# Eight value projections as four Winograd-style pairs ahead of the mixers, read back from DRAM

## The chip, the cores and the metric

The kernel runs on one core of a Trainium2 chip. The metric is the device time of one execution in microseconds (us), lowest is best. Engines: TensorE (PE) with its weight loads (PEld), VectorE (DVE), ScalarE (ACT), GpSimd (POOL), and SyncE (SP), which issues all of this kernel's DMAs in one queue of its own. Each engine works through its instructions strictly in order.

## The reference

One layer of a hybrid recurrent decoder: 1024 prompt tokens with 16 learned meta tokens ahead of them, and 8 sample sequences of 4 tokens, 1072 token columns in all, model width 1024. `w_in` makes everything that the four branches and the gates need, from the normalised input:

```python
xn = rmsnorm(h, norm_w)
(gq, gk, gv, glr, gg, hq, hf, hi, hg_g, mq, mk, mv, mi, mf, mo, mg,
 ca, cb, cg, mgate) = split_cols(xn @ w_in)
...
oA = chunked gated linear attention (q = gq, k = gk, v = gv, decay from glr)     # GLA, 4 heads, dk 64, dv 128
zA = head_rmsnorm(oA, gla_norm) * silu(gg)
oB = the same recurrence (q = silu(hq), k = 1 - f, v = hi, decay f from hf)      # HGRN2, 4 heads of 128
zB = head_rmsnorm(oB, hg_norm) * silu(hg_g)
zC = mLSTM branch (mq, mk, mv, mi, mf, mo, mg);  zD = convolution branch (ca, cb, cg)
...
mixed = sum over i of sigmoid(mgate_i) * (z_i @ w_branch[i])
h = h + mixed @ w_out;  y = rmsnorm(h, final_norm)
```

The mixers' states after the prompt and after each sample sequence are outputs too. `gv` and `hi`, the values of the first two branches, are 512 wide each: four blocks of 128 channels.

## The kernel before, in words

Data lie channels first: 128 channels by 1072 tokens (`NT`); the 1056 without meta tokens are `NY`, the 16 meta tokens `NM`. A float32 product is three matmuls of rounded parts, xh·wh, xl·wh and xh·wl (lines 185 to 187, and 280 to 282 in the pairs). ACT rounds the weights to `wh` (L138), POOL or DVE makes the rest `wl` (L139).

**Two ways to make a block of 128 output channels.** Direct (`proj`): three groups of 358, 358 and 356 columns (`GA`) or three of 352 (`GY`), each 8 slices of the depth by three products, 72 matmuls into a PSUM tile `acc`, and an eviction for each group. By pairs (`pair`): two neighbouring blocks at once, with seven half-size products in place of eight (Winograd's form of Strassen's scheme); 56 times three matmuls of at most 268 columns, 168 in all. The half sums of x are made once (`combine_x`), those of the weights for each pair (`ta`, `tb`), and DVE adds the partial sums up. `pair_to` applies a function and writes both blocks to a DRAM scratch (`gscr`, `cscr`, `sscr`), in quarters, without the meta columns.

**Stages.** x is normalised and transposed; four gate blocks and the small projections run directly. Then come 19 pairs in the order of the list `todo`, with the four convolution pairs and their 120 taps on DVE (L392) between the first. x is restored from scratch, and the mixers begin: `hg_unit` 0 to 3 (HGRN2, a head each), `gla_unit` 0 and 1 (GLA, two heads each), `ml_unit` 0 to 3. Last are the branch products and `w_out`.

**A mixer unit.** It projects its blocks directly (hf, hq and the value block hi for HGRN2; gk, gq and two value blocks gv for GLA). `vtok` makes the value block: three evictions by ACT into `vf` (one buffer, L589) and a copy of the sample columns `x9`; nine transposes on PE (`tta`, L546, PSUM tiles shared with `acc`, three buffers) and ACT's copies bring it to tokens first (`vt`, four buffers); one transpose `v9p` serves the samples. `linear_unit` then runs the scan in levels (`lv`, L647: PE, then DVE products q and k, L662 and L663), one or two filler gate blocks (`filler`), the state updates (`ds`, L812), the outputs (`op`, L831, L833, L733, L849), and at its end

- the norm: squares on ACT, sums on DVE (L774, L777), the power on POOL (L117), the product with o on DVE (L749, L751);
- `zt` (L755): nine transposes of o on PE, whose result DVE multiplies into the gate (L763, L758), and a write to `zscr`;
- `sds` (L860): the samples' state products, from masked values `vb` (L739), added to the states on DVE (L861), two for an HGRN2 head and four for a GLA unit.

`zt`, `sds`, `op`, `lv`, `ds` and `cps` come from one pool of three PSUM tiles. `ml_cols` (11 transposes `cps`, L981 to L994, each copied out by DVE) stands in the program between the two GLA units.

**What sets the order.** The program is written unit after unit. The framework's scheduler, with a timeline model of its own, puts every engine's instructions in one fixed list, and in it the end of a unit is interleaved with the next unit's projections:

```python
with tile.TileContext(nc, schedule_with_timeline_sim=True) as tc:
```

Of the kernel before, what the change touches and what calls it, by code (L numbers as in the profile page):

```python
# [12 lines left out]
F32 = mybir.dt.float32  # L13
# [3 lines left out]
AF = mybir.ActivationFunctionType  # L17
# [5 lines left out]
NM, NPR, NSEQ, NDEC = 16, 1024, 8, 4  # L23
NP = NM + NPR
NT = NP + NSEQ * NDEC
NY = NT - NM
D = 1024
P = 128
# [14 lines left out]
GA = [(0, 358), (358, 358), (716, 356)]  # L43
GY = [(16, 352), (368, 352), (720, 352)]
HT = NT // 2
# [20 lines left out]
def trunk(ctx, tc, hx, w_in, w_sm, w_br, w_out, pk, wgk2, mlb, fnorm, s_gla, s_hg, s_c, s_n, s_m, s_cv,  # L66
# [3 lines left out]
    V, S, G, T, DMA = nc.vector, nc.scalar, nc.gpsimd, nc.tensor, nc.sync  # L70

    cst = ctx.enter_context(tc.tile_pool(name="cst", bufs=1))
    dr = ctx.enter_context(tc.tile_pool(name="dr", bufs=1, space=DRAM))
# [39 lines left out]
    def mmt(name):  # L113
        return pools["pm"].tile([P, 512], F32, name=name, tag="mm")
# [9 lines left out]
    cscr = dr.tile([4, P, NY], F32, name="cscr", tag="cscr")  # L124
    xscr = dr.tile([2, P, KH, HT], F32, name="xscr", tag="xscr")
    sscr = dr.tile([16, P, NY], F32, name="sscr", tag="sscr")
    yscr = dr.tile([4, P, NY], F32, name="yscr", tag="yscr")

    def load_raw(src, c0, kd=KD):
        raw = pools["wp"].tile([P, KD, P], F32, name="wraw", tag="wraw")  # L130
        src = src if c0 is None else src[:, c0:c0 + P].rearrange("(k p) m -> p k m", p=P)
        DMA.dma_start(raw[:, :kd], src)
        return raw

    def split_w(raw, kd=KD, E=None, pool="wp"):
        hi = pools[pool].tile([P, KD, P], F32R, name="wh", tag="wh", bufs=2)
        lo = pools[pool].tile([P, KD, P], F32R, name="wl", tag="wl", bufs=2)
        S.activation(hi[:, :kd], raw[:, :kd], AF.Copy)  # L138
        (E or G).tensor_tensor(lo[:, :kd], raw[:, :kd], hi[:, :kd], ALU.subtract)  # L139
        return hi, lo  # L140

    def load_w(src, c0, kd=KD):
        return split_w(load_raw(src, c0, kd), kd)
# [5 lines left out]
    with tc.tile_pool(name="x0", bufs=9, side="right", reuse_waits="tile") as x0:  # L149
# [8 lines left out]
        for i0 in (0, 3, 6):  # L158
# [11 lines left out]
            for k in range(KD):  # L170
                ps = mmt("xt")
                t = 0
# [4 lines left out]
                hi = xh[:, k, i0 * P:i0 * P + t]  # L177
# [11 lines left out]
    def proj_w(hi, lo, groups, evac):  # L189
        for t0, n in groups:  # L190
            ps = acc_tile()
            mm3(ps[:, :n], lambda k: hi[:, k, :], lambda k: lo[:, k, :],
                lambda k: xh[:, k, t0:t0 + n], lambda k: xl[:, k, t0:t0 + n], KD)
            evac(ps[:, :n], t0, n)

    def proj(sec, i, groups, evac):
        hi, lo = load_w(w_in, OFF[sec] + i * P)
        proj_w(hi, lo, groups, evac)
# [9 lines left out]
    def stt(tag, name=None):  # L208
        return gtl(tag, [P, HT], STB[tag], name)
# [42 lines left out]
    def pair(c0, c1, c11, c12, c22, c21, m=0):  # L252

        wp = pools["gph"]
        r0, r1 = load_raw(w_in, c0), load_raw(w_in, c1)
        b11, b21, b12, b22 = r0[:, :KH], r0[:, KH:], r1[:, :KH], r1[:, KH:]
        w1 = split_w(r0)
        ta = wp.tile([P, KD, P], F32, name="ta", tag="tt", bufs=2)  # L260
        t1, t2 = ta[:, :KH], ta[:, KH:]
        V.tensor_tensor(t1, b12, b11, ALU.subtract)
        V.tensor_tensor(t2, b22, t1, ALU.subtract)
        w2 = split_w(ta, E=V, pool="gph")
        tb = wp.tile([P, KD, P], F32, name="tb", tag="tt", bufs=2)
        t3, t4 = tb[:, :KH], tb[:, KH:]
        V.tensor_tensor(t3, b22, b12, ALU.subtract)
        V.tensor_tensor(t4, b21, t2, ALU.subtract)
        w3 = split_w(tb, E=V, pool="gph")
        w4 = split_w(r1[:, KH:], KH)  # L270
        ps = lambda tag: [pools["ps"].tile([P, 512], F32, name="s" + tag, tag="a" if tag == "a" else "r",
                                           bufs=2 if tag == "a" else 5)[:, :HS] for _ in range(2)]

        def prod(w, o, x, s, out, start, stop, m=0):
            m = m if s == 0 else 0
            out = out[:, m:]
            xa, xb = (t[:, :, s * HS + m:(s + 1) * HS] for t in xs[x])
            for k in range(KH):
                wh, wl = w[0][:, o + k], w[1][:, o + k]
                T.matmul(out, wh, xa[:, k], start=start and k == 0, stop=False, skip_group_check=True)  # L280
                T.matmul(out, wh, xb[:, k], start=False, stop=False, skip_group_check=True)  # L281
                T.matmul(out, wl, xa[:, k], start=False, stop=stop and k == KH - 1, skip_group_check=True)  # L282

        h = lambda t, s: t[:, s * HS:(s + 1) * HS]
        a, b, c = ps("a"), ps("b"), ps("c")
        p1, u2 = stt("p1"), stt("u2")
        for s in range(2):
            prod(w1, 0, "a11", s, a[s], True, True)
            S.activation(h(p1, s), a[s], AF.Copy)
        for s in range(2):  # L290
            prod(w2, KH, "s2", s, b[s], True, True)
            V.tensor_tensor(h(u2, s), h(p1, s), b[s], ALU.add)
        p5, u3 = stt("p5"), stt("u3")
        for s in range(2):
            prod(w2, 0, "s1", s, c[s], True, True)
            S.activation(h(p5, s), c[s], AF.Copy)
        for s in range(2):
            prod(w1, KH, "a12", s, a[s], False, True, m)
            c11(s, a[s])
        d = ps("d")  # L300
        for s in range(2):
            prod(w3, 0, "s3", s, d[s], True, True)
            S.activation(h(u3, s), d[s], AF.Copy)
        V.tensor_tensor(u3, u3, p5, ALU.add)
        V.tensor_tensor(u3, u3, u2, ALU.add)
        c22(u3)
        for s in range(2):
            prod(w4, 0, "s4", s, c[s], False, True, m)
            V.tensor_tensor(h(p1, s), h(u2, s), c[s], ALU.add)
        c12(p1)  # L310
        for s in range(2):
            prod(w3, KH, "a22", s, d[s], False, True)
            V.tensor_tensor(h(u2, s), h(u2, s), d[s], ALU.add)
        c21(u2)

    def pair_to(sec, i, dst, func, times=False, base=0):

        g11 = stt("g11")
        o = OFF[sec] + i * P
        i += base  # L320

        def c11(s, ps):
            g = g11[:, s * HS:(s + 1) * HS]
            S.activation(g, ps, func)
            if times:
                V.tensor_tensor(g, ps, g, ALU.mult)  # L326
            if s == 1:
                DMA.dma_start(dst[i, :, 0:HT - NM], g11[:, NM:])

        def rest(j, second):  # L330
            def ev(t):
                if times:
                    sg = stt("sg")
                    S.activation(sg, t, func)
                    V.tensor_tensor(t, t, sg, ALU.mult)
                elif func != AF.Copy:
                    S.activation(t, t, func)
                if second:
                    DMA.dma_start(dst[j, :, HT - NM:], t)
                else:  # L340
                    DMA.dma_start(dst[j, :, 0:HT - NM], t[:, NM:])
            return ev

        pair(o, o + P, c11, rest(i + 1, False), rest(i + 1, True), rest(i, True), NM)

    def conv_pair(i):
        u = gtl("u", [P, UW + NSEQ * 34])
# [100 lines left out]
    for j in range(2, NDIR):  # L448
# [8 lines left out]
    todo = [("gate", i, gscr, AF.Sigmoid) for i in range(NDIR, 32 - NFILL, 2) if i not in LATE]  # L457
    todo += [("cg", i, cscr, AF.Copy) for i in (0, 2)]
    todo += [(sec, i, sscr, AF.Sigmoid, sec != "mo", 4 * n) for n, sec in ((3, "mo"), (0, "gg"), (1, "hg"), (2, "mg"))
             for i in (0, 2)]  # L460
    for i in range(4):
        cu = conv_pair(i)
        pair_to(*todo.pop(0))
        conv_taps(i, *cu)
        pair_to(*todo.pop(0))
        conv_states(i, *cu)
        pair_to(*todo.pop(0))
# [44 lines left out]
    for i in range(2):  # L512
        t = mx.tile([P, 8, P], F32, name=f"att{i}", tag=f"att{i}")
        G.memset(t, 0.0)
        attb.append(t)
        t = mx.tile([TAIL, TAIL], F32, name=f"att8{i}", tag=f"att8{i}")
# [6 lines left out]
    for i in range(2):  # L523
        t = mx.tile([TAIL, P], F32, name=f"attp{i}", tag=f"attp{i}")
# [58 lines left out]
    def vtok(sec, i, ones_col=False):  # L583
        vf = tl("vf", [P, 9 * P], 1)
        G.memset(vf[:, NT:NT + 16], 0.0)
        x9 = tl("x9", [P, 3, NT - NP], 1)

        def ev(ps, t0, n):
            S.activation(vf[:, t0:t0 + n], ps, AF.Copy)  # L589
            if t0 + n == NT:  # L590
                S.activation(x9, ps[:, NP - t0:].unsqueeze(1).broadcast_to([P, 3, NT - NP]), AF.Copy)

        proj(sec, i, GA, ev)
        vt = tl("vt", [P, 9, 129], 4)
        (to_tok_v(vf, vt) if ones_col else to_tok(vf, vt, True))
        v9 = split3(x9, 1, "v9", 4, mmt("v9p"))
        if ones_col:
            G.memset(vt[:, :, 128:129], 1.0)
        return vt, v9
# [669 lines left out]
    for i in range(9):  # L1269
# [24 lines left out]
        dst = yp[t0:t0 + P, :] if i < 8 else ys  # L1294
# [83 lines left out]
```

## Time and profile before

| what | value |
|---|---|
| median of 3 runs | 1569.58 us (1568.48 to 1570.25) |
| the profiled execution's own time | 1570.24 us |
| its span | 1568.5 us |
| mean granted clock of PE | 0.994 |
| instructions | 30293, of them 12471 matmuls |
| DMA | 176.43 MB, mean 112 GB/s |

The span runs from the first to the last instruction of the profiled execution, and the own time is what the device took for it; 1.7 us lie around the span. The page gives each engine's busy time as a share of the span, then the span in 40 slices of 39.2 us with a digit for the busy share, then the chain of work that ended last, and the groups of instructions by line. In rows such as `acc<-xh,wh` the written tile stands left of the arrow and the read ones right. Line numbers are those of the kernel before.

### The profile page before, as it was taken

What the parts mean: (1) busy time and instruction counts of PE and PEld (TensorE: products, weight loads), DVE (VectorE), ACT (ScalarE), POOL (GpSimd) and SP (SyncE); (2) the same over time, 40 slices, a digit from 0 to 9 for tenths busy, and PEclk for the clock granted to TensorE, in tenths of its full rate; (3) what the DMA queues carried; (4) which work ended last, traced back from release to release, by engine and by line L of the source; (5) the groups of instructions that cost most, each with busy time, mean ns of one, the idle gap of its engine ahead of it and who ended that gap; (6) DMA issues with size and microseconds to landing.
All of it is one profiled execution on the core that took longest, in us unless ns stands there. A gap on an engine that the chain in (4) does not pass through costs nothing. (4 is left out here: it accounts for less than half of the span.)

```text
span 1568.5 us, 30293 instructions
## 1 busy us (share of the span) xinstructions
PE 1530.4 (98%) x12471; PEld 1469.8 (94%) x12471; DVE 1039.6 (66%) x1825; ACT 558.8 (36%) x1131; POOL 465.5 (30%) x400
## 2 busy tenths in 40 slices
PE   6999999999999999999999999999999999999998
PEld 5999999999999999999998898999999999999886
DVE  6949989999998547445553666576675556744523
ACT  6543343332333334323522523423333255422311
POOL 2222222232213232223232222223323223877200
PEclk9999999999999999999999999999999999999999
DMA  5432333332337213231323133154333377676221
GB/s 175 136 99 76 97 110 103 96 110 71 95 106 230 56 44 111 57 104 52 109 69 101 37 92 91 58 151 127 110 96 93 105 251 212 189 240 192 95 106 49
DMA packets 195823, 176.43 MB, mean 112 GB/s; under 512 B 14508, under 2 KB 170048, under 8 KB 195684
## 3 DMA queue, kind: packets, MB, share of 16 engines
q1 hardware_dynamic: 195684, 174.49, 36.7%
q8 instruction: 98, 1.61, 0.4%
q14 instruction: 41, 0.34, 0.1%
HBM read 122.45 MB, written 52.00 MB: 111 GB/s over the span
## 5 line engine op out<-in xcount | busy, mean ns | idle before, releaser
L139 POOL TENSOR_TENSOR wl<-wraw,wh 128x512 fp32r<-128x512 f32 (+1 forms) x123 | 279.7, 2276 | 627.2 <-ACT wh L138 600.1
L185 PE MATMUL acc<-xh,wh 128*128 128x352 f32 (+2 forms) x1320 | 437.9, 332 | 2.2 <-ACT xh L178 2.2
L186 PE MATMUL acc<-xl,wh 128*128 128x352 f32 (+2 forms) x1320 | 436.0, 330 | 0.0
L187 PE MATMUL acc<-xh,wl 128*128 128x352 f32 (+2 forms) x1320 | 434.4, 329 | 0.0
L185 PEld LDWEIGHTS acc<-xh,wh 128*128 128x128 f32 x1320 | 250.6, 190 | 6.6 <-ACT xh L178 3.0
L186 PEld LDWEIGHTS acc<-xl,wh 128*128 128x128 f32 x1320 | 250.7, 190 | 1.9
L187 PEld LDWEIGHTS acc<-xh,wl 128*128 128x128 f32 x1320 | 250.2, 190 | 2.1 <-issue 0.7
L392 DVE SCALAR_TENSOR_TENSOR y<-u,pkt,y 128x1024 f32<-128x1024 f32 x120 | 192.7, 1606 | 0.6
L138 ACT ACTIVATE wh<-wraw 128x512 fp32r<-128x512 f32 (+1 forms) x125 | 110.4, 883 | 211.1 <-PE acc L186 116.5
L185 PE MATMUL acc<-zh,wh 128*128 128x352 f32 x384 | 124.6, 324 | 0.3 <-DVE gt L1209 0.3
L186 PE MATMUL acc<-zl,wh 128*128 128x352 f32 x384 | 124.4, 324 | 0.0
L187 PE MATMUL acc<-zh,wl 128*128 128x352 f32 x384 | 124.3, 324 | 0.0
L280 PE MATMUL sa<-xh,wh 128*128 128x268 f32 (+1 forms) x304 | 87.4, 287 | 1.7 <-DVE g L326 1.0
L281 PE MATMUL sa<-xl,wh 128*128 128x268 f32 (+1 forms) x304 | 86.6, 285 | 0.0
L282 PE MATMUL sa<-xh,wl 128*128 128x268 f32 (+1 forms) x304 | 86.6, 285 | 0.0
L1210 POOL TENSOR_TENSOR mix<-mix,gt 128x352 f32<-128x352 f32 x72 | 72.1, 1016 | 28.9 <-DVE gt L1209 25.7
L662 DVE TENSOR_TENSOR q<-q,tot 128x256 f32<-128x256 f32 (+3 forms) x96 | 45.8, 478 | 51.8 <-PE lv L647 51.1
L185 PEld LDWEIGHTS acc<-zh,wh 128*128 128x128 f32 x384 | 72.2, 188 | 1.1 <-issue 0.5
L187 PEld LDWEIGHTS acc<-zh,wl 128*128 128x128 f32 x384 | 72.3, 188 | 0.0
L186 PEld LDWEIGHTS acc<-zl,wh 128*128 128x128 f32 x384 | 72.2, 188 | 0.0
L1209 DVE TENSOR_TENSOR gt<-acc,gt 128x352 f32<-128x352 f32 x72 | 36.1, 517 | 38.6 <-PE acc L187 36.7
L280 PEld LDWEIGHTS sa<-xh,wh 128*128 128x128 f32 x304 | 57.3, 188 | 2.3 <-DVE g L326 1.4
(397 smaller groups left out, 3320.9 us busy)
## 6 DMA issues: line engine op xcount, KB each, us to landing
wraw<-w_in SPq DMA_DIRECT2D x92, 512.0 KB, 4.1
gt<-gscr SPq DMA_DIRECT2D x30, 528.0 KB, 4.9
gscr<-gd SPq DMA_DIRECT2D x60, 176.0 KB, 1.8
zr<-zscr SPq DMA_DIRECT2D x16, 528.0 KB, 4.3
wraw<-w_br SPq DMA_DIRECT2D x32, 256.0 KB, 2.9
gt<-sscr SPq DMA_DIRECT2D x12, 528.0 KB, 5.3
zscr<-gt SPq DMA_DIRECT2D x12, 528.0 KB
sscr<-u SPq DMA_DIRECT2D x16, 268.0 KB, 2.1
```

The costliest lines, as they stand in the source:

```text
L138: S.activation(hi[:, :kd], raw[:, :kd], AF.Copy)
L139: (E or G).tensor_tensor(lo[:, :kd], raw[:, :kd], hi[:, :kd], ALU.subtract)
L185: T.matmul(ps, wh(k), ah(k), start=(i == 0), stop=False)
L186: T.matmul(ps, wh(k), al(k), start=False, stop=False)
L187: T.matmul(ps, wl(k), ah(k), start=False, stop=(i == kd - 1))
L280: T.matmul(out, wh, xa[:, k], start=start and k == 0, stop=False, skip_group_check=True)
L281: T.matmul(out, wh, xb[:, k], start=False, stop=False, skip_group_check=True)
L282: T.matmul(out, wl, xa[:, k], start=False, stop=stop and k == KH - 1, skip_group_check=True)
L392: V.scalar_tensor_tensor(ymain, u[:, NM + j:NM + j + NPR], w(j), ymain, ALU.mult, ALU.add)
L662: V.tensor_tensor(qx[:, :, 1], qx[:, :, 1], pv[r, :, 0:1].broadcast_to([rw, nb, h]), ALU.mult)
L1209: V.tensor_tensor(gt[:, t0:t0 + n], ps[:, :n], gt[:, t0:t0 + n], ALU.mult)
L1210: G.tensor_tensor(mixed[j][:, t0:t0 + n], mixed[j][:, t0:t0 + n], gt[:, t0:t0 + n], ALU.add)
```

## The change

The eight value blocks of the HGRN2 and GLA units (`hi` and `gv`) are made in four more pairs, the last four of `todo`, with all 1072 columns (`m` = 0), and written to a new scratch `vscr`. `vtok` loads `vf` from there with one DMA of 128 x 1072 on SP's queue, and makes `x9` from `vf`; the direct projection stays for the mLSTM values alone. The number of weight blocks that are loaded, rounded and split stays the same. On PE 576 direct matmuls go and 672 of a pair's width come; ACT loses 24 evictions `vf<-acc`.

```diff
+    vscr = dr.tile([8, P, NT], F32, name="vscr", tag="vscr")
...
-    def pair_to(sec, i, dst, func, times=False, base=0):
+    def pair_to(sec, i, dst, func, times=False, base=0, m=NM):
...
-                DMA.dma_start(dst[i, :, 0:HT - NM], g11[:, NM:])
+                DMA.dma_start(dst[i, :, 0:HT - m], g11[:, m:])
...
-                    DMA.dma_start(dst[j, :, HT - NM:], t)
+                    DMA.dma_start(dst[j, :, HT - m:], t)
                 else:
-                    DMA.dma_start(dst[j, :, 0:HT - NM], t[:, NM:])
+                    DMA.dma_start(dst[j, :, 0:HT - m], t[:, m:])
...
-        pair(o, o + P, c11, rest(i + 1, False), rest(i + 1, True), rest(i, True), NM)
+        pair(o, o + P, c11, rest(i + 1, False), rest(i + 1, True), rest(i, True), m)
...
+    VB = {"hi": 0, "gv": 4}
+    todo += [(sec, i, vscr, AF.Copy, False, VB[sec], 0) for sec in VB for i in (0, 2)]
...
-        proj(sec, i, GA, ev)
+        if sec in VB:
+            DMA.dma_start(vf[:, :NT], vscr[VB[sec] + i])
+            S.activation(x9, vf[:, NP:NT].unsqueeze(1).broadcast_to([P, 3, NT - NP]), AF.Copy)
+        else:
+            proj(sec, i, GA, ev)
```

The rows of the order below carry the changed kernel's own line numbers, which are up to 7 higher (`zt` L762 for L755, `tta` L549 for L546, `lv` L654 for L647, the products L186 to L188 for L185 to L187), and numbers behind the names that count tiles; behind a row stands what it waits for.

**The end of an HGRN2 unit, on PE.** The first unit's last output matmul is followed, before, by 63 matmuls of projections, the next unit's value block among them; then its `zt`:

```order
L187 MATMUL acc_6700<-xh_96,wl_6643 128x352
L185 MATMUL acc_6700<-xh_96,wh_6642 128x352
L186 MATMUL acc_6700<-xl_97,wh_6642 128x352
L755 MATMUL zt_6470<-ident_70,o_6420 128x128 [waits DVE_49,PE_49]
L755 MATMUL zt_6470<-ident_70,o_6420 128x128 x3
```

In the changed kernel 40 matmuls of projections and eight transposes of the next unit's loaded value block stand there:

```order
L187 MATMUL acc_7526<-xl_98,wh_7468 128x352
L188 MATMUL acc_7526<-xh_97,wl_7469 128x352
L549 MATMUL tta_7561<-ident_70,vf_7555 128x128 [waits DMAHW6_49,DVE_49]
L549 MATMUL tta_7561<-ident_70,vf_7555 128x128 x3
L549 MATMUL tta_7567<-ident_70,vf_7555 128x128 [waits DVE_49]
L549 MATMUL tta_7567<-ident_70,vf_7555 128x128 x3
L762 MATMUL zt_7296<-ident_70,o_7246 128x128 [waits DVE_49,Activation_49]
L762 MATMUL zt_7296<-ident_70,o_7246 128x128 x3
```

Behind the second and the third unit's outputs it was 51 and 61 matmuls, and is 30 and 42 with eight transposes.

**The two value blocks of the first GLA unit, on PE.** Before, the transposes of the first block (`vf_9334`) are followed by the 72 matmuls of the second block, of which the first few are shown, and only then by its transposes:

```order
L546 MATMUL tta_9435<-ident_70,vf_9334 48x128 [waits Activation_49]
L565 MATMUL v9p_9438<-ident_70,x9_9336 96x128 [waits PE_49]
L185 MATMUL acc_9452<-xh_96,wh_9448 128x358 [waits Activation_49]
L186 MATMUL acc_9452<-xl_97,wh_9448 128x358
L187 MATMUL acc_9452<-xh_96,wl_9449 128x358 [waits Pool_49]
```

Now the load of the second block (`vf_9937`, into the one buffer that `vf_9911` held) has the rest of the level and the fourth HGRN2 unit's `zt` ahead of its transposes:

```order
L549 MATMUL tta_9929<-ident_70,vf_9911 48x128 [waits Activation_49]
L654 MATMUL lv_10017<-q_9722,k_9733 32x32 [waits DVE_49]
L654 MATMUL lv_10017<-q_9722,k_9733 32x32 x9
L762 MATMUL zt_9689<-ident_70,o_9639 128x128 [waits DVE_49]
L762 MATMUL zt_9689<-ident_70,o_9639 128x128 x3
L762 MATMUL zt_9695<-ident_70,o_9639 128x128 [waits DVE_49]
L762 MATMUL zt_9695<-ident_70,o_9639 128x128 x3
L762 MATMUL zt_9701<-ident_70,o_9639 128x128 [waits DVE_49]
L549 MATMUL tta_9943<-ident_70,vf_9937 128x128 [waits DMAHW0_49]
```

In the second GLA unit the second load stands likewise, with 31 `lv`, two `ds` and seven `op` of the first unit in between, and the first unit's other 35 outputs behind it.

**The end of the first GLA unit, on PE.** Before, its state products and the `cps` transposes are spread over the next unit's two value blocks; each `sds` has projection matmuls ahead of it and behind it:

```order
L186 MATMUL acc_10578<-xl_97,wh_10522 128x356
L187 MATMUL acc_10578<-xh_96,wl_10523 128x356
L185 MATMUL acc_10578<-xh_96,wh_10522 128x356
L860 MATMUL sds_10174<-vb_10175,k9_10000 128x512 [waits DVE_49,PE_49]
L981 MATMUL cps_10180<-ident_70,ct_6506 128x96 [waits PE_49]
```

Now they follow each other:

```order
L867 MATMUL sds_10570<-vb_10571,k9_10411 128x512 [waits DVE_49]
L867 MATMUL sds_10575<-vb_10576,k9_10411 128x512 [waits DVE_49]
L867 MATMUL sds_10580<-vb_10581,k9_10411 128x512 [waits DVE_49,PE_49]
L867 MATMUL sds_10585<-vb_10586,k9_10411 128x512 [waits DVE_49,PE_49]
L988 MATMUL cps_10591<-ident_70,ct_7332 128x96 [waits PE_49]
L988 MATMUL cps_10594<-ident_70,ct_7332 128x96 [waits DVE_49]
L988 MATMUL cps_10597<-ident_70,ct_7332 128x96 [waits DVE_49]
```

## The prediction

> **What bounds the kernel now.** The page comes first: busy shares, the slices of the span, the chain that ended last.
>
> ```profile
> span 1568.5 us, 30293 instructions
> PE 1530.4 (98%) x12471; PEld 1469.8 (94%) x12471; DVE 1039.6 (66%) x1825; ACT 558.8 (36%) x1131; POOL 465.5 (30%) x400
> PE   6999999999999999999999999999999999999998
> DVE  6949989999998547445553666576675556744523
> PE 23%; DVE 1%; DMA 1%; issue 0%; ACT 0%; DVEq 0%; POOLq 0%; SPq 0%; POOL 0%; ACTq 0%
> ```
>
> TensorE (PE) is busy in 98% of the span, in every slice but the ends, and the part of the chain that the profile follows is PE's. So two sums count: how many matmul columns go away, and how long PE stands still in its fixed order at the places from which they are taken. DVE is full in the first 12 slices (pairs and convolution) and half idle in the mixers. Then come PE's timeline for the price of a pair and of a direct block, and the timelines of PE, DVE and POOL where a unit ends, for what the removed blocks covered. Rows give start, duration, line, operation, and in brackets the idle time before with its releaser.
>
> **The change part by part.** *Pairs against direct blocks.*
>
> ```profile
> 473.73 0.39 PE L280 MATMUL sa<-xh,wh 128*128 128x268 f32 x1 [0.50 <-DVE g L326]
> 494.44 0.33 PE L185 MATMUL acc<-xh,wh 128*128 128x358 f32 x1
> 506.24 0.33 PE L185 MATMUL acc<-xh,wh 128*128 128x352 f32 x1
> 517.83 0.33 PE L185 MATMUL acc<-xh,wh 128*128 128x358 f32 x1
> 529.61 0.27 PE L546 MATMUL tta<-ident,vf 128*128 128x128 f32 x1
> ```
>
> The last pair runs from 473.73 to 494.44: 20.71 us for two blocks. The three direct blocks of the first unit follow, the third its value block: 529.61 − 517.83 = 11.78 us. Eight value blocks leave the mixers: 8 × 11.78 = 94.2 us. Four pairs are added. With the meta columns kept, 24 of their 168 matmuls have 268 columns instead of 252, 24 × 16 columns at the 358 columns per 0.164 us of a direct block (11.78 / 72) = 0.18 us, so 4 × 20.9 = 83.6. PE gains **10.6 us** (10 to 12: the larger end is the columns, 25,728 fewer, at that rate). DVE, full when the earlier pairs ran, has no taps left beside the new ones; ACT's roundings and POOL's or DVE's weight splits stay as many and move ahead. The scratch writes and the eight loads go through SP's queue, which is no bound there. I cost these at nothing: their cover is the 20.9 us of each pair, and if the new pairs became DVE's they would cost as in the last rival. The first unit's block is written three pairs earlier, and two direct blocks (23 us) stand between.
>
> *End of an HGRN2 unit.* Between a unit's last output matmul and the transposes of its normalised output (zt), PE had the next unit's value block. Now 40, 30 and 42 projection matmuls and eight transposes stand there (63, 51 and 61 matmuls before). What it must cover:
>
> ```profile
> 654.39 0.49 PE L849 MATMUL op<-vt,attp 48*128 48x128 f32 x2
> 655.21 1.28 DVE L774 TENSOR_REDUCE ms<-sq 128x4 f32<-128x512 f32 x2 [4.47 <-ACT sq L773]
> 656.60 0.17 DVE L777 TENSOR_SCALAR ms<-ms 128x9 f32<-128x9 f32 x1
> 656.85 1.81 POOL L117 TENSOR_TENSOR ms<-ms,mhalf 128x9 f32<-128x9 f32 x1 [0.57 <-DVE ms L777]
> 658.69 3.49 DVE L749 TENSOR_TENSOR o<-o,ms 128x512 f32<-128x512 f32 x2 [1.92 <-POOL ms L117]
> 659.05 2.59 POOL L139 TENSOR_TENSOR wl<-wraw,wh 128x1024 fp32r<-128x1024 f32 x1 [0.39 <-ACT wh L138]
> 662.11 0.27 DVE L751 TENSOR_SCALAR o<-o,ms 128x128 f32<-128x128 f32 x1
> 663.16 1.03 PE L755 MATMUL zt<-ident,o 128*128 128x128 f32 x8
> 806.38 0.48 PE L849 MATMUL op<-vt,attp 48*128 48x128 f32 x2
> 816.27 0.27 DVE L751 TENSOR_SCALAR o<-o,ms 128x128 f32<-128x128 f32 x1
> ```
>
> From the end of op (the rows show it at 654.88) the normalised output takes until 662.38, 7.5 us; in the fourth unit 806.86 to 816.54, 9.7. PE's new cover is 40 × 0.164 + 8 × 0.13 (eight transposes in 1.03) = 7.6, then 6.0 and 7.9 us. The waits are 0 + 1.5 + 0 with the short chain and 2.1 + 3.7 + 1.8 with the long one: 1.5 to 7.6 us for the three. I take **3.5**, nearer the short one, since in the fourth unit scan steps stood inside DVE's chain. Below nothing it can't go, since PE had work there. Behind the waiting zt stand the unit's state products and the next unit's matmuls; DVE waits for zt (gate product, L763).
>
> *Two reloads in the GLA units.* The value tile vf has one buffer. A GLA unit has two value blocks, so the second load (on SP) is issued only when PE has transposed the first, and the transposes of the second (tta) stand a few instructions later. SP waits there too, and what it holds back (weights, states) is wanted later than the block itself.
>
> ```profile
> gt<-gscr SPq DMA_DIRECT2D x30, 528.0 KB, 4.9
> gt<-sscr SPq DMA_DIRECT2D x12, 528.0 KB, 5.3
> zr<-zscr SPq DMA_DIRECT2D x16, 528.0 KB, 4.3
> 850.26 0.66 PE L546 MATMUL tta<-ident,vf 128*128 128x128 f32 x4 [0.84 <-ACT vf L589]
> 864.17 0.46 PE L647 MATMUL lv<-q,k 128*32 128x32 f32 x32 [1.92 <-DVE k L663]
> 911.10 0.39 PE L831 MATMUL op<-vt,att 128*128 128x128 f32 x2
> 911.32 0.39 PE L833 MATMUL op<-sall,q 128*128 128x128 f32 x2
> ```
>
> Loads of this size from scratch land 4.3 to 5.3 us after issue; I take 4.9, and 0.27 for the last transpose to end. In the first GLA unit PE has 10 lv (0.15) and nine zt (1.15 at most) in between: 5.17 − 1.2 = **4.0 us** idle (3.4 to 4.4), the fourth HGRN2 unit's zt wait included. In the second GLA unit 31 lv (0.45), two ds and seven op (0.11 each, by 911.10 to 911.32 for two) are 1.45: **3.7 us** (3.1 to 4.1), and the other 35 outputs of the first unit are queued behind. Before, both had a projection of 11.78 us there and waited only for ACT's eviction, 0.84 us in the first unit, which goes (0.8 in the sum). A load can't come sooner than its buffer is free, so neither falls below its end.
>
> *State products of the first GLA unit.* Four sds and eleven transposes cps stood among the matmuls of the next unit's two value blocks. Now they stand in a row. Each needs a PSUM tile (three) that DVE must empty:
>
> ```profile
> 929.94 1.59 DVE L763 SCALAR_TENSOR_TENSOR gt<-zt,pkt,gt 128x496 f32<-128x496 f32 x2
> 931.54 0.39 DVE L758 SCALAR_TENSOR_TENSOR gt<-zt,pkt,gt 128x16 f32<-128x16 f32 x2
> 933.77 0.68 DVE L861 TENSOR_TENSOR s<-s,sds 64x512 f32<-64x512 f32 x1 [1.83 <-PE sds L860]
> 934.37 0.68 DVE L739 TENSOR_TENSOR vb<-v,vmask 96x512 fp32r<-96x512 f32 x1
> 943.68 0.25 DVE L982 COPY cols<-cps 128x12 f32<-128x12 f32 x2 [0.69 <-PE cps L981]
> 945.13 0.25 PE L989 MATMUL cps<-ident,x 96*128 96x96 f32 x1
> ```
>
> DVE has, behind the last zt, 2.0 for the gate, 4 × 0.68 sums, 2 × 0.68 masks and 11 × 0.12 copies: 7.4 us, while PE has 4 × 0.23 (512 columns at the rate above) + 11 × 0.11 = 2.1. PE idles about **5.2 us** (3.5 if gate and masks are done early, 7 with 0.2 us of handing over at eight of the steps).
>
> *The clock.* Windows of 2 us: length, busy time and count of PE, PEld, DVE, ACT, POOL, then the granted clock:
>
> ```profile
> 862.00:864.00 2.00, 0.25 (x2) 0.00 (x0) 1.97 (x4) 1.06 (x1) 0.00 (x0) 1.00 0.00 0
> 864.00:866.00 2.00, 0.46 (x32) 0.35 (x32) 1.94 (x7) 1.97 (x3) 0.87 (x4) 0.85 0.01 4
> 866.00:868.00 2.00, 1.95 (x38) 1.91 (x39) 1.72 (x6) 1.94 (x3) 0.29 (x3) 0.50 0.03 8
> 868.00:870.00 2.00, 2.00 (x8) 2.00 (x8) 1.94 (x7) 1.98 (x2) 0.01 (x1) 0.50 0.00 0
> 870.00:872.00 2.00, 2.00 (x8) 2.00 (x8) 1.22 (x6) 0.65 (x2) 0.00 (x0) 0.50 0.23 87
> 872.00:874.00 2.00, 2.00 (x74) 1.74 (x73) 0.37 (x1) 0.75 (x1) 0.00 (x0) 0.94 0.01 4
> ```
>
> After 4 us with PE at 0.71 us of work, the clock was 0.50 until about 872. From 867 that is 5 us at half speed, 2.5 us lost. The two reloads and the state products each leave PE as empty for about as long, so I add 3 × 2.5 = **7.5 us** (2.5 to 7.5). The Trainium skill (TensorE: Matmul & The Clock Gate, Part 1) ties the drop to a whole idle window of about 3.4 us, free-running, and here the clock fell over two windows that held 0.71 us of matmuls, so the rule is stricter than this row. By that rule waits of 3.7 to 5.2 us would seldom cover a whole window, and the sum would be the second rival's instead of mine.
>
> **The sum:** −10.6 − 0.8 + 3.5 + 4.0 + 3.7 + 5.2 + 7.5 = **+12.5 us**. The profiled execution took 1570.24 us, 0.66 above the median; the difference is carried over to the median: 1569.58 + 12.5 = **1582.1**. With every term at its good end: −12 − 0.8 + 1.5 + 3.4 + 3.1 + 3.5 + 2.5 = +1.2; at its bad end −10 − 0.8 + 7.6 + 4.4 + 4.1 + 7 + 7.5 = +19.8. So the forecast's own range is 1571 to 1589.
>
> **The rivals.** *Faster: DVE catches up in the new waits.* PE already waits in the mixers for the scan's products:
>
> ```profile
> PE lv L647 <- DVE k L663: 8.6, 7, 1.9
> ```
>
> If DVE works on while PE stands still, and POOL's weight splits no longer run beside it at the units' ends (the 3.49 us of L749 for two had such a split beside it), the later waits shrink: up to 8.6, and the two clock drops that they cause, 5.0. With the low ends of the new waits, no drop of the clock and half of those 13.6 gained, −10.6 − 0.8 + 1.5 + 3.4 + 3.1 + 3.5 − 6.8 = −6.7: 1563. Against it: the lv waits are serial, PE to DVE to PE within one unit, and a head start is used up at the first level. It decides if waits and clock together cost under 11.4 us.
>
> *Waits without the clock drops:* 12.5 − 7.5 = +5.0, 1574.6. For it: the drop in the windows followed two waits, and no row of before shows a single one of 4 us. Against it: PE did as good as nothing in either case.
>
> *Longer waits:* the long chain at all three HGRN2 ends (+4.1), with a drop at two of them (+5.0): +21.6, 1591. For it speaks the fourth unit's 9.7 us; against it, that these waits come singly.
>
> *The gain doesn't come:* the new pairs are held by DVE or by their writes, and cost what eight direct blocks do: +23.1, 1592.7. DVE's slices of 9 while the pairs run speak for it; against it that the taps of the convolution end with the earlier pairs.
>
> *Nothing to see:* the waits at their low ends, no drops, nothing gained later: +0.1, 1569.7.
>
> **How the numbers follow.** The measurement can't tell 0.2% (3.1 us) from no change, so "same" is 1566.4 to 1572.7. Chances: forecast 0.46, waits without drops 0.19, longer waits 0.08, no gain 0.05, nothing to see 0.09, faster 0.13. The forecast's and the second's good ends give another 0.02 to "same". Faster 0.13, same 0.11, slower 0.76. For 8 in 10 I leave out most of "faster" and the upper halves of the two dear rivals: 1566 to 1592.
>
> **What would show it.** Right: four more pairs of 20 to 21.5 us each before the mixers; tta of the second value block in both GLA units waiting 3 to 5 us for the DMA vf<-vscr; the sds and cps of the first GLA unit spread over 7 to 10 us with PE mostly idle; zt in units two and three waiting 1 to 4 us for DVE's o; windows with a granted clock of about 0.5 behind the reloads and the state products; PE's share below 98%. Wrong: pairs of more than 22 us; PE busy at those places because the lists are late for another reason; an L663 wait total well under 8.6; a clock of 1.00 behind waits of 4 us.

## The result, and the profile after

The changed kernel takes 1588.7 us (median of 4 runs, 1584.43 to 1592.36) against 1569.28 before: a ratio of 1.0124, 95% interval [1.0112, 1.0136], some 19.4 us slower. The profiled execution took 1584.43 us, the shortest of the four, 14.2 above the profiled one of before. Its page, the lines that stood in the prediction for the kernel before:

```profile
span 1582.5 us, 30670 instructions
PE 1527.1 (96%) x12567; PEld 1463.5 (92%) x12567; DVE 1070.0 (68%) x1881; ACT 567.1 (36%) x1148; POOL 460.0 (29%) x400
PE   6999999999999999999999898999999999999998
PE 70%; DVE 17%; DMA 5%; issue 3%; ACT 1%; SPq 0%; POOL 0%; DVEq 0%; POOLq 0%; ACTq 0%
```

PE does less (1527.1 us busy for 1530.4) in a longer span, so it stands still for 55.4 us instead of 38.1. Two 8s stand among its 9s. The chain that ended last runs over DVE for 17% and over DMA for 5%; before, the profile could follow the chain over only a quarter of the span, so these shares can't be compared with those of before. Three windows of the kernel before, 800 to 900, 900 to 1000 and 1250 to 1300 us (length, busy time and count of PE, PEld, DVE, ACT, POOL, then the granted clock):

```profile
800.00:900.00 100.00, 94.19 (x1004) 89.83 (x1002) 52.20 (x109) 36.23 (x72) 29.25 (x28) 0.97 0.23 66
900.00:1000.00 100.00, 96.11 (x1040) 90.17 (x1037) 60.49 (x144) 31.35 (x72) 25.16 (x22) 0.98 0.27 78
1250.00:1300.00 50.00, 50.00 (x319) 49.85 (x318) 25.57 (x41) 24.90 (x45) 9.23 (x8) 1.00 0.80 249
```

The same of the changed kernel:

```profile
800.00:900.00 100.00, 90.53 (x1138) 85.39 (x1137) 55.80 (x121) 41.39 (x70) 26.61 (x30) 0.94 0.39 118
900.00:1000.00 100.00, 89.54 (x1109) 81.77 (x1108) 63.86 (x166) 28.92 (x70) 22.93 (x23) 0.92 0.25 77
1250.00:1300.00 50.00, 46.48 (x279) 45.00 (x278) 21.20 (x38) 19.67 (x43) 10.85 (x8) 0.97 0.63 197
```

Here both losses are to be seen side by side. In these three windows PE stands still for 23.5 us of 250 instead of 9.7, and the lowered clock takes 15.5 us (0.06 × 100 + 0.08 × 100 + 0.03 × 50) instead of 5. The gain came as forecast. PE's timeline after, at the start of the first added pair and behind the last:

```profile
492.21 0.29 PE L281 MATMUL sa<-xh,wh 128*128 128x268 f32 x1
575.43 0.33 PE L186 MATMUL acc<-xh,wh 128*128 128x358 f32 x1
```

Four pairs in 83.2 us, 20.8 each. Where PE then waits, in the order of time (start, duration, in brackets the wait before and its releaser):

```profile
600.87 0.29 PE L549 MATMUL tta<-ident,vf 128*48 128x128 f32 x1 [0.89 <-ACT vt L550]
666.24 0.30 PE L762 MATMUL zt<-ident,o 128*128 128x128 f32 x1 [1.67 <-DVE ig L960]
818.03 0.45 PE L654 MATMUL lv<-q,k 128*32 128x16 f32 x32 [1.36 <-DVE k L670]
867.93 2.18 PE L762 MATMUL zt<-ident,o 128*128 128x128 f32 x9 [2.07 <-DVE o L756]
869.90 1.65 PE L549 MATMUL tta<-ident,vf 128*128 128x128 f32 x9
929.44 0.71 PE L838 MATMUL op<-vt,att 128*128 128x128 f32 x4
931.20 0.27 PE L654 MATMUL lv<-q,k 128*32 128x32 f32 x8
932.42 1.20 PE L549 MATMUL tta<-ident,vf 128*128 128x128 f32 x9 [0.96 <-DMA vf<-vscr]
941.30 0.43 PE L186 MATMUL acc<-xh,wh 128*128 128x352 f32 x1 [1.12 <-ACT vt L550]
955.41 0.49 PE L867 MATMUL sds<-vb,k 96*128 96x512 f32 x1 [0.28 <-DVE gt L770]
958.27 0.47 PE L867 MATMUL sds<-vb,k 96*128 96x512 f32 x1 [1.70 <-DVE vb L746]
959.70 0.77 PE L867 MATMUL sds<-vb,k 96*128 96x512 f32 x1 [0.95 <-DVE vb L746]
961.25 1.73 PE L988 MATMUL cps<-ident,ct 96*128 96x96 f32 x7 [0.46 <-DVE s L868]
1280.36 0.42 PE L186 MATMUL acc<-zh,wh 128*128 128x352 f32 x1 [1.17 <-ACT zh L1201]
1281.65 0.43 PE L187 MATMUL acc<-zl,wh 128*128 128x352 f32 x1 [0.87 <-DVE zl L1202]
1283.84 0.59 PE L187 MATMUL acc<-zl,wh 128*128 128x352 f32 x1 [0.87 <-DVE zl L1202]
```

None of these waits is longer than 2.1 us, there are many, and they reach to the start of the branch products, some 700 us behind the first place from which a block was taken. The level products wait a little more than before in sum (10.6 us in 6 waits for 8.6 in 7), but the longest of them is 3.7 us instead of 1.9:

```profile
PE lv L654 <- DVE k L670: 10.6, 6, 3.7
```

### The profile page after: what moved, and what is told of

Its sections match the earlier page's. It is cut to its first block, busy times and chain, and to the rows that moved or that the text cites. A ratio compares the mean times of both kernels' runs of the same rounds, so it can differ in the third digit from the quotient of the medians.

```text
span 1582.5 us, 30670 instructions
## 1 busy us (share of the span) xinstructions
PE 1527.1 (96%) x12567; PEld 1463.5 (92%) x12567; DVE 1070.0 (68%) x1881; ACT 567.1 (36%) x1148; POOL 460.0 (29%) x400
## 4 chain that ended last, share of the span: by engine, by line
PE 70%; DVE 17%; DMA 5%; issue 3%; ACT 1%; SPq 0%; POOL 0%; DVEq 0%; POOLq 0%; ACTq 0%
PE acc L187 15%; PE acc L186 15%; PE acc L188 15%; DVE y L393 6%; PE lv L654 2%; PE sc L281 2%; PE sc L282 2%; PE sc L283 2%; PE sa L282 2%; PE sa L281 2%; PE sa L283 2%; DMA wraw<-w_in 2%; PE sd L281 1%; PE sd L282 1%; PE sd L283 1%
## 5 line engine op out<-in xcount | busy, mean ns | idle before, releaser
L186 PE MATMUL acc<-xh,wh 128*128 128x352 f32 (+2 forms) x1128 | 374.7, 333 | 4.6 <-ACT xh L179 3.0
L187 PE MATMUL acc<-xl,wh 128*128 128x352 f32 (+2 forms) x1128 | 374.4, 332 | 0.0
L188 PE MATMUL acc<-xh,wl 128*128 128x352 f32 (+2 forms) x1128 | 373.0, 331 | 0.0
L186 PEld LDWEIGHTS acc<-xh,wh 128*128 128x128 f32 x1128 | 215.1, 191 | 8.4 <-ACT xh L179 3.9
L187 PEld LDWEIGHTS acc<-xl,wh 128*128 128x128 f32 x1128 | 214.9, 191 | 2.6 <-issue 0.3
L188 PEld LDWEIGHTS acc<-xh,wl 128*128 128x128 f32 x1128 | 214.7, 190 | 2.0 <-issue 0.3
L187 PE MATMUL acc<-zl,wh 128*128 128x352 f32 x384 | 125.2, 326 | 1.7 <-DVE zl L1202 1.7
L186 PE MATMUL acc<-zh,wh 128*128 128x352 f32 x384 | 125.3, 326 | 1.6 <-ACT zh L1201 1.5
L188 PE MATMUL acc<-zh,wl 128*128 128x352 f32 x384 | 125.0, 325 | 0.0
L281 PE MATMUL sa<-xh,wh 128*128 128x268 f32 (+1 forms) x368 | 105.7, 287 | 1.7 <-DVE g L327 1.0
L282 PE MATMUL sa<-xl,wh 128*128 128x268 f32 (+1 forms) x368 | 105.0, 285 | 0.0
L283 PE MATMUL sa<-xh,wl 128*128 128x268 f32 (+1 forms) x368 | 105.0, 285 | 0.0
L669 DVE TENSOR_TENSOR q<-q,tot 128x256 f32<-128x256 f32 (+3 forms) x96 | 50.4, 525 | 55.4 <-PE lv L654 54.6
L186 PEld LDWEIGHTS acc<-zh,wh 128*128 128x128 f32 x384 | 72.8, 190 | 2.9 <-ACT zh L1201 2.1
L187 PEld LDWEIGHTS acc<-zl,wh 128*128 128x128 f32 x384 | 72.8, 189 | 2.3 <-DVE zl L1202 2.2
L188 PEld LDWEIGHTS acc<-zh,wl 128*128 128x128 f32 x384 | 72.8, 190 | 0.0
L282 PEld LDWEIGHTS sa<-xl,wh 128*128 128x128 f32 x368 | 69.4, 189 | 0.0
```

Of the source, the lines that this page charges most:

```text
L186: T.matmul(ps, wh(k), ah(k), start=(i == 0), stop=False)
L187: T.matmul(ps, wh(k), al(k), start=False, stop=False)
L188: T.matmul(ps, wl(k), ah(k), start=False, stop=(i == kd - 1))
L669: V.tensor_tensor(qx[:, :, 1], qx[:, :, 1], pv[r, :, 0:1].broadcast_to([rw, nb, h]), ALU.mult)
```

## The experiments

Theory: the value blocks were PE's work while DVE, POOL and the loads did the units' serial steps; without them PE waits at those steps, and its clock falls. Rivals: the values' new way (DRAM, SP's queue, the one buffer) costs; or the GLA units alone are tight. All runs below are against the kernel before, on the same chip (medians 1568.6 to 1569.3).

**1. The cover put back.** The eight direct projections are computed too, and dropped (the tile `gd`, which other places share, grows from 352 to 358 columns for it).

```diff
             S.activation(x9, vf[:, NP:NT].unsqueeze(1).broadcast_to([P, 3, NT - NP]), AF.Copy)
+
+            def drop(ps, t0, n):
+                S.activation(tl("gd", [P, 358], 1, name="vdrop")[:, :n], ps, AF.Copy)
+
+            proj(sec, i, GA, drop)
...
```

> As the changed kernel, but the eight direct projections stay where they were in the units, their results evicted by ACT into a tile that nobody reads; the values still come through DRAM. It does the work of both kernels, so its time is read against before + four pairs (83.3 us in the profile after) = 1652.6 us. Theory (lost cover: the waits came because PE had nothing else to do while DVE, POOL and the loads worked): the waits at zt, sds, cps and tta and the extra clock drops go away again, 1650 to 1656 us. Rival (the way through DRAM, the queue of SP and ACT's copies cost by themselves): the 19 us of the change stay, 1668 to 1674 us.

1651.75 us, ratio 1.0527 [1.0513, 1.0542]: 82.6 above before, the price of the four pairs alone. Its page:

```profile
span 1649.9 us, 31909 instructions
PE 1612.9 (98%) x13143; PEld 1552.0 (94%) x13143; DVE 1075.1 (65%) x1881; ACT 586.4 (36%) x1180; POOL 475.2 (29%) x408
```

With 94.2 us of useless matmuls more it is only 63 us slower than the changed kernel: some 31 us of them cost nothing. PE's waits of over 0.1 us behind 480 us come to 10.4 us, for 11.6 before and 28.7 in the changed kernel. The way through DRAM costs nothing that can be seen while PE has that work. The theory holds, and the rival that the way costs by itself falls.

**2 to 4. Which unit pays.** More filler for the GLA units, and the values of one branch alone (`VB = {"hi": 0}`, `VB = {"gv": 4}`).

```diff
-        for _ in range(3 - nh):
+        for _ in range(2):
             filler()
...
-        for _ in range(3 if h == 3 else 1):
+        for _ in range(1):
             filler()
```

> As the changed kernel, but each GLA unit has two filler gate blocks instead of one, and the last mLSTM unit one instead of three. The same matmuls, 2 x 11.6 us of them moved into the two GLA units. Theory (lost cover): the GLA units' waits (in the profile after 0.9 + 0.6 + 3.7 and 0.5 + 3.7 for the level products, 1.0 for the second block, 3.4 at sds and cps) and three of the clock's drops shrink by half or more: 1574 to 1582 us. Rival (these waits are serial between PE and DVE, and what is taken from the last mLSTM unit is missed there): 1586 to 1594 us.

1603.71 us, 1.0218 [1.0204, 1.0232]: 15 slower than the changed kernel: a miss of the theory in the form that I gave it, and 10 us beyond the rival's range too. The waits of the GLA units were not filled, and the last mLSTM unit lost its own cover:

```profile
899.05 0.66 PE L654 MATMUL lv<-q,k 128*32 128x32 f32 x32 [3.73 <-DVE k L670]
1282.83 2.52 PE L762 MATMUL zt<-ident,hc 128*128 128x128 f32 x9 [6.53 <-DVE hc L753]
```

The scheduler put about 23 projection matmuls between two level products in both kernels; a block more in the program went behind the levels, not into the wait.

> Only the HGRN2 values in pairs (two more pairs), the GLA values direct as before. Gain of PE 2 x (23.56 - 20.8) = 5.5 us. Theory (each unit pays where its own cover went): the HGRN2 waits of the profile after (0.9 tta, 1.7 + 1.4 + 2.1 zt, 0.4 sds, 1.8 level products, one drop of the clock 1.7) come and the GLA units' don't: 1569.3 - 5.5 + 8 = 1572 (1568 to 1576). Rival (the loss sits in the GLA units through what the HGRN2 units hand on: their clock drops and DVE's lateness come anyway): 1578 to 1585.

1569.32 us, 1.0001 [0.9992, 1.0010]: no change, as the theory said. Of the 5.5 us of gain 4.4 are to be found again as waits: 16.0 us of waits over 0.1 us on PE behind 480 us, for 11.6 before. The new ones stand where they stand in the changed kernel; the rest of the gain isn't accounted for:

```profile
560.75 0.29 PE L549 MATMUL tta<-ident,vf 128*48 128x128 f32 x1 [0.89 <-ACT vt L550]
626.12 0.30 PE L762 MATMUL zt<-ident,o 128*128 128x128 f32 x1 [1.67 <-DVE ig L960]
```

> Only the GLA values in pairs (two more pairs). Gain of PE 5.5 us. Theory (each unit pays where its own cover went): the waits of the GLA units (1.0 tta, 1.1 for ACT's vt, 3.4 sds and cps, 2.1 zt of the unit before, some 1 more at the level products) and three drops of the clock (7): 1569.3 - 5.5 + 15 = 1579 (1574 to 1584). Rival (the clock's drops were there before at the same products and the waits only moved): 1566 to 1571.

1591.25 us, 1.0145 [1.0130, 1.0161]: 22 slower, beyond both ranges, more than the theory's 10 and no less than the whole change (19.4). With the HGRN2 blocks in place the fourth unit's zt is done early, and both reloads stand bare. SP's issue of the first one, PE's waits, and three windows of 2 us:

```profile
865.70 0.32 SPq L597 DMA_DIRECT2D vf<-vscr  x1
871.57 2.18 PE L549 MATMUL tta<-ident,vf 128*128 128x128 f32 x9 [5.59 <-DMA vf<-vscr]
PE tta L549 <- DMA vf<-vscr: 9.3, 2, 5.6
868.00:870.00 2.00, 0.00 (x0) 0.00 (x0) 1.71 (x4) 0.00 (x0) 0.00 (x0) 0.55 1.03 365
870.00:872.00 2.00, 0.43 (x2) 0.44 (x3) 0.00 (x0) 0.28 (x1) 0.00 (x0) 0.50 0.65 182
876.00:878.00 2.00, 2.00 (x8) 2.00 (x8) 1.97 (x2) 0.28 (x1) 2.00 (x2) 0.50 0.41 163
```

One wait of 5.6 us, and the clock is at 0.50 until 878, six microseconds into full work. Its lowered stretches in the mixers and at the branches' start add up to 41 us by the trace's record of the clock, 20.5 lost, for 5.1 before.

**5 and 6. The loads and cps moved earlier.** In the one the vtok calls of each GLA unit stand a unit earlier and `ml_cols(ct)` ahead of the fourth HGRN2 unit; in the other `ml_cols(ct)` alone.

```diff
...
     hg_unit(2)
+    ml_cols(ct)
+    vts0 = [vtok("gv", i) for i in range(2)]
     hg_unit(3)
...
-    gla_unit(0)
-    ml_cols(ct)
-    gla_unit(1)
+    nxt_vts = []
+    gla_unit(0, vts0, 1)
+    gla_unit(1, nxt_vts)
```

> As the changed kernel with all eight values in pairs, but each GLA unit's two value blocks are loaded and transposed one unit earlier in the program (the first unit's ahead of the fourth HGRN2 unit, the second's inside the first GLA unit ahead of its scan), and the cps transposes stand ahead of the fourth HGRN2 unit. Theory (the loss of the GLA values is the reload of vf and the row of sds and cps, made dearer by the clock): 1.0 + 0.3 for the second blocks, half of the 3.4 + 0.5 at sds and cps and one or two drops of the clock go: 1578 to 1583 us against 1588.7. Rival (the loss is the missing PE work under the serial chain between PE and DVE, wherever the loads stand): within 3 us of 1588.7 or slower.

1591.52 us, 1.0144 [1.0129, 1.0160]: no gain, as the rival said. The reload only waits elsewhere, inside the fourth HGRN2 unit and inside the first GLA unit:

```profile
816.93 2.18 PE L549 MATMUL tta<-ident,vf 128*128 128x128 f32 x9 [4.99 <-DMA vf<-vscr]
887.85 2.15 PE L549 MATMUL tta<-ident,vf 128*128 128x128 f32 x9 [3.17 <-DMA vf<-vscr]
```

> As the changed kernel, but the 11 cps transposes of ml_cols stand ahead of the fourth HGRN2 unit in the program. If PE's wait at the first GLA unit's end is DVE's row of sums and copies, cps's 0.5 us and DVE's 1.3 us of copies leave it: 1 to 3 us less than 1588.7. If sds alone waits (for vb and the gate), no change: 1588 to 1590.

1584.36 us, 1.0098 [1.0083, 1.0113]: 4.3 below the changed kernel's median, and level with the shortest of its four runs (1584.43). The wait at the first GLA unit's end is gone; zt of the fourth HGRN2 unit waits 5.15 us instead of 2.07, and that of the last mLSTM unit 3.5. So it says nothing sure of cps's own price.

**7, 8 and 12. The mLSTM values.** `VB = {"mv": 0}`, `VB = {"hi": 0, "mv": 4}`, and the first of these with one filler moved from the first HGRN2 unit to the last mLSTM unit.

> Two more pairs, for the four mLSTM values (mv) instead of the HGRN2 and GLA ones. PE gains the same 5.5 us. The mLSTM units show 0.5 us of PE idle in all in the profile before. Theory (what decides is whether a unit's own cover lasts, and one block of 11.8 us of three goes here): 2 to 4 us come back as waits, 1566 to 1568. Rival (every value block that is taken out of a unit costs what it gains, as with hi): 1569 to 1571.

1585.66 us, 1.0106 [1.0090, 1.0123]. A miss of both, by size: the stage that showed half a microsecond of idle PE loses 17. The end of the last unit had its cover in these blocks:

```profile
1243.01 3.88 PE L1070 MATMUL dc<-vt,kwt 128*128 128x129 f32 x18 [2.48 <-POOL kwt L1060]
1263.91 2.53 PE L762 MATMUL zt<-ident,hc 128*128 128x128 f32 x9 [8.59 <-DVE hc L753]
```

> Four more pairs as in the changed kernel, but for the HGRN2 and the mLSTM values; the GLA values stay direct. PE gains 10.9 us. If the loss of the change sits in the GLA units alone, this is faster than before: hi gave 0, mv 2 to 4: 1565 to 1569. Rival (it is the number of blocks taken out of the mixers that counts, and the scheduler has nothing left to fill with): 1575 to 1590.

1590.7 us, 1.0138 [1.0123, 1.0153]: the rival. Four pairs more cost 22 us here too, with the GLA values direct.

> As the run with the mLSTM values alone in pairs, with one filler moved from the first HGRN2 unit to the last mLSTM unit (four there). The zt of the last unit waited 8.6 us and dc 2.5, with 10 us of lowered clock behind (5 lost). Theory (cover at the last unit's end decides): the block of 11.6 us fills most of that and 1585.7 becomes 1570 to 1575. Rival (the order puts the block elsewhere, as with the GLA fillers): 1583 to 1590.

1592.03 us, 1.0147 [1.0132, 1.0162]: the rival again. The filler was not where it was needed: zt still waits 8.58 us.

**9 to 11. The same saving without any value.** The kernel before, with filler blocks in pairs instead.

```diff
-    NFILL = 16
+    NFILL = 8
...
-        for _ in range(3 - nh):
+        for _ in range(2 - nh):
...
-        for _ in range(3 if h == 3 else 1):
+        for _ in range((0, 0, 1, 3)[h]):
```

> The kernel before with all values direct, and eight of the 16 filler gate blocks in four more pairs instead: one filler left for each HGRN2 unit, none for the GLA units, and 0, 0, 1 and 3 for the mLSTM units. PE gains 4 x (2 x 11.59 - 20.71) = 9.9 us, and no value goes through DRAM. Theory (it is the PE work taken out of the mixers that costs, whatever it makes): as slow as the changed kernel, 1580 to 1600. Rival (the values' own way, load and buffer, costs): the gain stays, 1559 to 1566.

1601.51 us, 1.0205 [1.0190, 1.0221]: 32 slower, worse than the change, with no value in DRAM and no reload. The largest wait stands where the mLSTM runs had it:

```profile
1278.53 2.52 PE L755 MATMUL zt<-ident,hc 128*128 128x128 f32 x9 [8.58 <-DVE hc L746]
```

So for these blocks the loss belongs to the PE work taken out of the mixers, whatever that work makes.

The wait doesn't stand where the work was taken out, though. In this run the last mLSTM unit still has its three fillers, and in run 12 it has four. What counts is what the fixed list puts at that place. Between the unit's last state product (`sdn`) and its `zt`, the traces show 71 projection matmuls in the kernel before and in runs 1, 3, 10 and 11, and `zt` doesn't wait. They show 64 in the changed kernel and in runs 4 and 5, again without a wait; 17 in run 6, with 3.5 us; and none in runs 2, 7, 8, 9 and 12, with 6.5 to 8.6 us. In those five the list has spent what is left earlier. (The changed kernel's own waits stand elsewhere, as listed with its profile.) Whether the same work in a better order would lose less is open: runs 2, 5, 6 and 12 moved blocks in the program, and no run set the list itself.

> The kernel before with two filler blocks fewer (one less in the first two HGRN2 units) and one more gate pair. PE gains 23.18 - 20.71 = 2.5 us. If the first two HGRN2 units have cover to spare, 1566 to 1567.5; if the mixers have none left anywhere, 1569 to 1573.

1570.35 us, 1.0010 [1.0001, 1.0018]: no gain, in the range for mixers without cover to spare.

> The kernel before with four filler blocks fewer (one less in each HGRN2 unit) and two more gate pairs. PE gains 4.9 us. If the HGRN2 units have cover to spare (their values in pairs came out even), 1564 to 1567; if not, 1569 to 1575.

1568.8 us, 0.9998 [0.9990, 1.0007]: between the two ranges. Two and four fillers out of the HGRN2 units bring nothing and cost nothing, like their four values in run 3. In the second a new wait of 2.57 us (`v9p` behind DVE's sums, at 642 us) took part of the 4.9 us of gain; idle time and lowered clock together were as before there, so the rest isn't accounted for. No version was measured faster than before.

## Why the prediction was right, and where its terms were off

1588.7 lies in the range (1566 to 1592), the sign is right, and the likeliest case with its own range (1571 to 1589) holds it at its upper end. The sum was +12.5; the profiled executions differ by 14.0 in span (PE 3.3 us less busy, 17.3 more idle), and the medians by 19.4. That 12.5 and 14.0 lie so close is partly luck. The waits that I priced came to 9.7 us in place of 16.4, and 7.3 us of waits that I hadn't priced made up for it.

- **Pairs, −10.6:** 83.2 us for four, against 83.6. Right: DVE and the writes, costed at nothing, didn't hold the new pairs. (DVE isn't full in all of its first 12 slices, as I wrote; its digits there include a 6 and a 4.)
- **zt of the first three HGRN2 units, +3.5:** 1.67 and, in the second, 1.43, none in the third: 3.1. The sum is nearly right, the places and the reason aren't. In both units the wait is for the last part of o (L758), which took 2.37 us beside one of POOL's weight splits; in the third unit, without a split, it took 0.28:

```profile
663.56 2.45 POOL L140 TENSOR_TENSOR wl<-wraw,wh 128x1024 fp32r<-128x1024 f32 x1 [1.06 <-ACT wh L139]
663.72 2.37 DVE L758 TENSOR_SCALAR o<-o,ms 128x128 f32<-128x128 f32 x1
795.61 0.28 DVE L758 TENSOR_SCALAR o<-o,ms 128x128 f32<-128x128 f32 x1
```

  (The releaser named for the first wait, `ig`, is the instruction behind it on DVE.) The kernel before has this too, 2.40 and 2.42 us in the first and the third unit, under PE's cover; my rows were those of the second and the fourth.
- **Reloads, +4.0 and +3.7:** 2.07 (all of it zt, the load came by then) and 0.96. The mechanism is real, run 4 shows 5.59 and 3.71. But I took the time of one matmul record for that of one product. Each of these float32 products (`lv`, `ds`, `op`) is two records: the order lists seven `op` there, and the trace has 14 records of them, 929.44 to 931.20, 1.76 us and not 0.77. With the 31 `lv` and two `ds` PE had 3.1 us of work from 928.33 on, where I counted 1.45. And the load came sooner: issued at 928.43, it released PE at 932.42, 4.0 us later, where I took 4.9. The step that failed is the count of what lies between, for 1.7 of the 2.7 us by which the second wait was too long; most of the rest is the load.
- **sds and cps, +5.2:** 0.28 + 0.16 + 1.70 + 0.95 + 0.46 = 3.55 (the 0.16 isn't shown above). That it meets my low end is luck: the 3.5 doesn't follow from its terms, since 7.4 us of DVE less 2.0 for the gate and 1.4 for the masks leaves 4.0 against 2.1 on PE. What happened is something else. DVE did half of the gate's products while zt still ran, and three of the masks (`vb`) stood in the row: 1.70 and 0.95 are waits for them.
- **The clock, +7.5:** in the three windows +10.5. Of the three places that I named, two had a lowered stretch (3.4 us at the first reload, 6.8 at the state products) and the second reload had none. It fell not only behind the long waits but behind 1.36 us with small level products around it (819 us), and at the branches' start. Against that, the kernel before has a lowered stretch near its start, as the traces of all other kernels here do, that this execution hasn't: windows 20 to 40 of before and of after,

```profile
20.00:40.00 20.00, 16.64 (x88) 13.72 (x87) 14.70 (x30) 11.79 (x22) 2.79 (x4) 0.83 0.15 45
20.00:40.00 20.00, 16.71 (x103) 13.89 (x101) 17.55 (x36) 12.81 (x24) 2.75 (x4) 1.00 0.28 95
```

  0.17 × 20 = 3.4 us that the change didn't bring.
- **Not priced at all:** the first unit's third transposes (0.89), the fourth unit's level products (1.36 and 0.46), ACT's vt ahead of the second GLA unit (1.12), and 3.5 us at the branches' start. These 7.3 us have no term in the sum, because I priced only the places next to the removed blocks. The mixers' list is one chain, and what PE no longer has to do in one unit is missing at its end too.
- **Rivals.** DVE's catching up didn't happen (10.6 us of level waits for 8.6). Waits without drops of the clock: no. Missing gain: no. The longer waits: not longer ones, but more of them. Of the signs that I gave for being right, two didn't come: the second value blocks didn't wait 3 to 5 us for the load (0 and 0.96), and PE wasn't mostly idle at sds and cps (3.6 us of 7.8). That the difference of the medians is 5 us above the profiled one goes in the main with the clock: the four executions were granted 0.989 (the profiled one), 0.987, 0.986 and 0.984 on the mean, those of the kernel before 0.992 to 0.997.

The Trainium skill (TensorE: Matmul & The Clock Gate, Part 1) ties the drop to a whole idle window of about 3.4 us. The traces differ: waits of 1.4 to 2.1 us with sparse work around them did it. Half speed agrees, and so does a window of that length, since the lowered stretches are 3.4 and 6.8 us long (10.2 in run 4, over six of them behind the wait, and 13.7 in run 12). By such a window a wait of 5.2 us would cover a whole one about every second time, as an estimate, so "seldom" was too strong for it. The weighing in favour of the row was right.

## What to carry to other kernels

A kernel whose PE is 98% busy can still be held by serial steps on other engines, with the PE work as their cover: saving matmuls there pays only up to the cover that is to spare (here four blocks of the HGRN2 units, and even they for nothing). Before such a saving, put the work back as a dummy beside it: as much of the dummy as is free was cover and not PE's bound. Count in each kernel's own list what stands ahead of a serial step, since a block moved in the program need not arrive there. Price the waits at every serial step downstream and not only beside the edit, and count a matmul's records in the trace, not its rows in an order.

## What was not expected of the hardware

A short wait can have a second price. In the changed kernel six lowered stretches of the clock, 30.7 us in all between 819 and 1288 us by the trace's record, came with waits of 0.9 to 3.7 us, the short ones in groups (before: 10.2 us in two stretches), each 3.4 or 6.8 us long, at 0.50. The waits of 0.89, 1.67 and 1.43 us at 601, 666 and 734 us had none. In run 4 the clock's 15.4 us more are the larger part of what was lost (22.1 us and the gain of 5.5).

A product of DVE can last until POOL's split beside it ends. The last part of o took 0.27 or 0.28 us in 88 of the 112 cases of the 14 traces. In the other 24 a weight split of POOL had begun before it and still ran; it took 2.36 to 2.45 us, and ended 0.1 us behind the split. Why it does so is not shown.
